# Eight convolution taps of two channel groups as ScalarE products and GpSimd sums

## The chip, the core and the metric

The kernel runs on one core of a Trainium2 chip. Its engines have queues of their own and meet through semaphores: TensorE (PE, with its weight loads PEld), VectorE (DVE), ScalarE (ACT), GpSimd (POOL) and SyncE (SP, which issues the DMAs). The metric is the device time of one launch, in microseconds (us).

## The reference, cut to what matters

Two layers over 256 frames of 1024 channels. In each layer the input projection feeds two things: attention on one half, and on the other half a Conformer convolution module over 512 channels. The part that the change touches is the causal depthwise convolution of width 31:

```
def conformer_conv(u, conv_w, conv_b, ln_g, ln_b):
    a, g = jnp.split(u, 2, axis=-1)
    z = a * jax.nn.sigmoid(g)
    z = lax.conv_general_dilated(
        z, conv_w, window_strides=(1,), padding=[(CONV_WIDTH - 1, 0)],
        dimension_numbers=("NWC", "WIO", "NWC"),
        feature_group_count=D_CONV) + conv_b
    z = layernorm(z, ln_g, ln_b)
    return jax.nn.silu(z)
...
y = jnp.concatenate([y_conv, y_att], axis=-1) @ w_out[l]
x = x + g1[:, None, :] * y
```

Layer 0 then has a dense SwiGLU, layer 1 a top-2-of-8 expert SwiGLU. All data are float32.

## The kernel before

`mix(l, ...)` is the first half of layer `l`: projection, convolution, attention, output projection. Channels lie on the 128 partitions, frames along the free axis. The 512 convolution channels are four groups `a` = 0 to 3 of 128 channels. `glu(a, ps)` takes a projected pair out of PSUM: a sigmoid on ACT (`sg`, line 584) and a product on DVE (line 585) that writes `zp[:, a]`, the padded convolution input. From there each of the 31 taps of a group is one DVE instruction on 128x256: the first a `tensor_scalar` with the bias (line 547), the others `cv = zp shifted * weight + cv` (line 550), with both tensors in SBUF. Of group 3 the last taps (15 in layer 0, 19 in layer 1) are matmuls on PE against diagonal matrices `dgc`, which ACT makes from the identity (line 565); `pe_taps` (line 570) issues them and `pe_done` (line 577) adds their sum.

The whole stretch is under a manual schedule: each engine runs its instructions in the order in which the code is written. The taps are spread by hand. `pump(n)` issues the next `n` taps that are left, taking turns between groups, and `pt(i)` calls it at thirteen marked places with counts from the tables `PUMP0` and `PUMP1`; the `tap` hook puts one tap between the steps of a reciprocal square root in `qk_norm`. What is left is flushed by `pump(4 * CW)` on line 831, ahead of `ln_mean`, where PE averages `cv` over channels (`ps_mu`, line 678).

Between those places stand, in this order: the q and k projections (`ps_q`, `ps_k`) with their norms `qk_norm` (DVE, `qh`), the transposes to `qT` and `kT` (PE `ps_qt`, ACT line 609), the groups 2 and 3 of the convolution input, three blocks of scores (`ps_s`) with their softmax (DVE line 631 gives `s_sb` and the maximum `nm`; ACT line 636 the exponentials), the v projection (`ps_v`), then on ACT the diagonals `dgc`, on PE the transposes `ps_pt`, the taps `ps_cv`, and the weighted sums `ps_o`, which DVE normalises to `o_sb` (line 666). Weights come as 1 MB pieces `raw` by DMA; ACT rounds each to `hi` (line 146) and DVE takes the rest `lo = raw - hi` (line 154, both inputs in SBUF). The four-slot and seven-slot pools `a8` and `a4` hold the larger tiles; `T` is the position bias, loaded by DMA, of which POOL overwrites a corner (line 760).

Of the kernel before, what the change touches and what calls it, by code (L numbers as in the profile page):

```python
# [13 lines left out]
AF = mybir.ActivationFunctionType  # L14
ALU = mybir.AluOpType
AX = mybir.AxisListType

P = 128
D = 1024
S = 256  # L20
# [4 lines left out]
CW = 31  # L25
NE = 8
NPE = (15, 19)
FILL = (1, 1, 1, 0, 1, 10)
NDVE = 9
PT0 = (52, 13, 23, 22)  # L30
PT1 = (29, 49, 15, 36)
RAW = 9
# [21 lines left out]
def kernel(ctx, tc, x, cvec, wada, bada, wga, wqkv, wout, wfgu, wfd, wfd2,  # L54
                      wmgu, wmd, cols, bias, wrt, brt, out):
    nc = tc.nc
# [10 lines left out]
    def bank(name):  # L67
        return pb.tile([P, 512], F32, tag="b", name=name)
# [6 lines left out]
    def sized(tag):  # L75
        def f(name, shape, dt=F32):
            return pools["wk"].tile(shape, dt, tag=tag, name=name, bufs=bufs[tag])
        return f

    a8, a4, a2 = sized("a8"), sized("a4"), sized("a2")  # L80
# [77 lines left out]
    for l in range(2):  # L158
        first = (wqkv[l, 0], wga[l, 0]) if l else (wga[l, 0], wqkv[l, 0])
# [59 lines left out]
    def ahead(nhi, nlo=None, pre=True):  # L219

        for _ in range(nhi):
            if len(his) < limit[0]:
                k, s = halves[len(his)]
                need(k + pre)
                his.append(half_hi(raws[k], s))
            else:
                need(len(raws) + pre)
        for _ in range(nhi if nlo is None else nlo):
            if len(los) < limit[0]:
                k, s = halves[len(los)]  # L230
                los.append(half_lo(raws[k], s, his[len(los)]))
# [50 lines left out]
    ada_raw = []  # L282
    ada_order = [(0, c) for c in (2, 0, 3, 1, 4, 5, 6, 7, 8, 9, 10, 11)] + [(1, c) for c in range(NDVE, 12)]
    ada_done = [0]
# [39 lines left out]
    def ada_through(n):  # L324
        ada_next(n - ada_done[0])
        ada_flush()
# [9 lines left out]
    def ada_steps(l, chs):  # L336

        steps, ws, accs = [], {}, {}

        def fetch(ch):  # L340
            if ch in chs:
                ws[ch] = ada_view(load(wada[l, ch]))

        def part(ch, j):
            if j == 0:
                if ch == chs[0]:
                    fetch(ch)
                accs[ch] = a2("ada_acc", [P, 512])
                nc.vector.tensor_scalar(accs[ch], ws[ch](0), cs[:, 0:1], None, op0=ALU.mult)
            else:  # L350
                if j == 4:
                    fetch(ch + 1)
                nc.vector.scalar_tensor_tensor(accs[ch], ws[ch](j), cs[:, j:j + 1], accs[ch], op0=ALU.mult,  # L353
                                               op1=ALU.add)

        def total(ch):
            ps = bank("ps_adas")
            for g in range(4):
                nc.tensor.matmul(ps[32 * g:32 * g + 32, 0:P], ones_1[:, 0:32], accs[ch][:, g * P:(g + 1) * P],
                                 start=True, stop=True)  # L360
            ada_rows(l, ch, ps)

        for ch in chs:
            for j in range(KT):
                steps.append(lambda ch=ch, j=j: part(ch, j))
                if j == 6 and ch > chs[0]:
                    steps.append(lambda ch=ch: total(ch - 1))
        return steps, lambda: total(chs[-1])
# [14 lines left out]
    def vec(l, v):  # L383
        return vcol[:, l, 2 * v:2 * v + 2, :].rearrange("p a b -> p (a b)")

    def scale_col(l, v, ng, name):
        a = const.tile([P, KT], F32, name=name)
        for q in range(2):
            s = slice(4 * q, 4 * q + 4)
            nc.vector.scalar_tensor_tensor(a[:, s], vec(l, v)[:, s], 1.0, ng[:, s], op0=ALU.add, op1=ALU.mult)  # L390
        return a
# [139 lines left out]
    def mix(l, late, close, hhi, hlo, head=None):  # L531
        zp = a8("zp", [P, 4, S + CW - 1])
        nc.gpsimd.memset(zp[:, :, 0:CW - 1], 0.0)
        cv = a4("cv", [P, 4, S])
        cw = COL["cw", l].rearrange("p (a i) -> p a i", a=4)
        taps, turn = {}, [0]

        def pump(n):

            for _ in range(n):  # L540
                left = [a for a in taps if taps[a]]
                if not left:
                    return
                a = max(left, key=lambda a: (a != turn[0], len(taps[a])))
                turn[0], i = a, taps[a].pop(0)
                if i == 0:
                    nc.vector.tensor_scalar(cv[:, a, :], zp[:, a, 0:S], cw[:, a, 0:1], COL["cb", l][:, a:a + 1],
                                            op0=ALU.mult, op1=ALU.add)
                else:
                    nc.vector.scalar_tensor_tensor(cv[:, a, :], zp[:, a, i:i + S], cw[:, a, i:i + 1], cv[:, a, :],  # L550
                                                   op0=ALU.mult, op1=ALU.add)
# [26 lines left out]

        def pt(i):
            pump((PUMP0, PUMP1)[l][i])  # L580

        def glu(a, ps):
            sg = a2("sg", [P, S])
            nc.scalar.activation(sg, ps[:, 0], AF.Sigmoid)
            nc.vector.tensor_tensor(zp[:, a, CW - 1:], ps[:, 1], sg, op=ALU.mult)
            taps[a] = list(range(CW - NPE[l] if a == 3 else CW))

        def qk_norm(bk):
            ss = sm.tile([P, NT, H], F32, tag="qss", name="qss")
# [50 lines left out]
        def turned(qt, h0, hg, s_sb):  # L640
            nkb = qt + 1
            r = []
            for b0 in range(0, hg * nkb, 4):
                ps = bank("ps_pt").rearrange("p (a s) -> p a s", a=4)
                for a in range(4):
                    h, kb = divmod(b0 + a, nkb)
                    nc.tensor.transpose(ps[:, a, :], s_sb[:, h, kb * P:(kb + 1) * P], ident)
                pT = a2("pT", [P, 4, P])
                nc.scalar.activation(pT, ps, AF.Copy)
                r.append((b0, pT))  # L650
            return r
# [23 lines left out]
        def ln_mean():  # L675
            ps = bank("ps_mu")
            for a in range(4):
                nc.tensor.matmul(ps[:, 0:S], ones_m, cv[:, a, :], start=a == 0, stop=a == 3)
            nc.vector.tensor_tensor(cv, cv, ps[:, None, 0:S].to_broadcast([P, 4, S]), op=ALU.subtract)
            sq = a4("sqc", [P, 4, S])  # L680
            nc.scalar.activation(sq, cv, AF.Square)
            return sq
# [110 lines left out]
        for t in range(NT):  # L793
            nc.scalar.activation(v_sb[:, t, :], bv[t], AF.Copy)
        n0, n1, n2, n3 = (PT0, PT1)[l]
        p0 = turned(*g0, s0)
# [32 lines left out]
        ahead(1, 0)  # L829
        ada_through(6)  # L830
        pump(4 * CW)
        sq = ln_mean()
        ahead(0, 1)
        out_att(wa, (0,))
# [13 lines left out]
    def ffn(hhi, hlo, late):  # L848
# [18 lines left out]

        steps, last = ada_steps(1, range(NDVE))
        total, done = len(steps), [0]
# [511 lines left out]
    def late_mix1():  # L1381
        ada_through(22 - NDVE)
        A, B = scale_col(1, 4, COL["ng2", 1], "A2_1"), vec(1, 3)
        nc.vector.tensor_scalar(A, A, NORM, None, op0=ALU.mult)
        BW = a2("BW", [P, KT, NE])
        for o_, v in ((BW, B), (wrt_sb, A)):
            nc.vector.tensor_tensor(o_, wrt_sb, v[:, :, None].to_broadcast([P, KT, NE]), op=ALU.mult)
        ps = bank("ps_bw")
        nc.tensor.matmul(ps[:, 0:KT * NE], ones_1, BW.rearrange("p j e -> p (j e)"), start=True, stop=True)
        bw = const.tile([P, NE], F32, name="bw")  # L1390
        nc.vector.tensor_reduce(bw, ps[:, 0:KT * NE].rearrange("p (j e) -> p e j", e=NE), axis=AX.X, op=ALU.add)
        nc.vector.tensor_tensor(bw, bw, brt_sb, op=ALU.add)
        return A, B, wrt_sb, bw
# [10 lines left out]
    with tc.manual_schedule():  # L1404
# [45 lines left out]
        ga(w0, *dst, p0, ((0, range(4, 8)), (1, range(8))))  # L1450
        ga(w1, *dst, p1, ((0, range(4, 8)), (1, range(8))))
        mix(0, keep(late_mix0), close_block, *dst, (p0, p1, bq))
        ffn(*dsts[0], keep(late_ffn))
        nc.sync.dma_start(wrt_sb, wrt)
# [3 lines left out]
        def close_mix1(*args):  # L1458
            layer2.append(moe(*args))
            next(layer2[0])  # L1460

        mix(1, late_mix1, close_mix1, *dsts[1])
    next(layer2[0], None)

# [56 lines left out]
```

## Time and profile before

| | us |
|---|---|
| median of 3 runs | 1393.73 (1391.57 to 1395.06) |
| profiled execution | 1396.89 |
| its span, first to last instruction | 1395.2 |
| PE busy | 1322.7 (95%) |
| DVE busy | 772.2 (55%) |
| ACT busy | 371.5 (27%) |
| POOL busy | 3.1 (18 instructions) |

The busy shares are means over the whole span. The two mixes lie at about 47 to 165 us and 387 to 505 us; the rest is the dense SwiGLU between them and the experts behind them. In the rows below a time is counted from the start of the span.

### The profile page before, as it was taken

Reading aid. Unit: us, or ns where it says so; the run is one execution under the profiler, and the core shown is the slowest. Engines: PE = TensorE matmul, PEld = TensorE weight load, DVE = VectorE, ACT = ScalarE, POOL = GpSimd, SP = SyncE. Lnnn points to the kernel's source line nnn. Section 1 sums busy time; section 2 is a strip of 40 time slices with the busy share of each in tenths; the row PEclk is TensorE's granted clock in tenths of the full one; section 3 lists DMA queues with packets and bytes.
Section 4 is the critical chain, followed back from the end, with each engine's and each line's share of the span. In section 5 each row is a group of like instructions: output and inputs, shape, how many; then the busy total and the mean of one; then the engine's idle time right before and its main releaser. Section 6 shows DMA issues by size and latency. Waiting matters only on the chain.

```text
span 1395.2 us, 38875 instructions
## 1 busy us (share of the span) xinstructions
PE 1322.7 (95%) x17220; PEld 974.2 (70%) x17220; DVE 772.2 (55%) x1832; ACT 371.5 (27%) x574; POOL 3.1 (0%) x18
## 2 busy tenths in 40 slices
PE   4998999999899999999899999999999999999996
PEld 4877689999788676666567666766765776666663
DVE  3498677777689855343566565653344343334253
ACT  3336443443455430101234333410000100100000
POOL 0000000000000000000000000000000000000000
PEclk9999999999999999999999999999999999999999
DMA  9962787888461469899879999999999999999995
GB/s 387 399 276 91 262 305 275 307 300 300 161 237 59 151 218 401 353 424 424 344 309 423 387 373 371 367 413 424 424 425 424 424 424 424 396 418 418 423 424 215
DMA packets 66383, 473.64 MB, mean 339 GB/s; under 512 B 7840, under 2 KB 7968, under 8 KB 9248
## 3 DMA queue, kind: packets, MB, share of 16 engines
q1 hardware_dynamic: 66208, 471.09, 83.9%
q8 instruction: 137, 2.24, 0.6%
q14 instruction: 38, 0.31, 0.1%
HBM read 470.01 MB, written 1.05 MB: 338 GB/s over the span
## 4 chain that ended last, share of the span: by engine, by line
PE 81%; DVE 8%; DMA 6%; ACT 4%; issue 1%; SPq 0%; ACTq 0%; DVEq 0%
PE ps_gu L1090 28%; PE ps_d L1090 14%; PE ps_ga L262 4%; PE ps_ga L260 4%; PE ps_ga L261 4%; DMA raw<-in_wmd 3%; DVE lo L154 3%; PE ps_g L1031 2%; PE ps_y L714 2%; PE ps_ada L314 2%; DVE hT L1135 1%; PE ps_f L261 1%; PE ps_f L260 1%; PE ps_f L262 1%; PE ps_gu L262 1%; DMA raw<-in_wmgu 1%
## 5 line engine op out<-in xcount | busy, mean ns | idle before, releaser
L1090 PE MATMUL ps_gu<-raw,xn 128*32 128x256 f32 x8064 | 445.8, 379 | 1.2 <-DVE rt L983 0.6
L1090 PEld LDWEIGHTS ps_gu<-raw,xn 128*32 128x32 f32 x8064 | 279.3, 110 | 156.1 <-issue 2.4
L154 DVE TENSOR_TENSOR lo<-raw,hi 128x2048 fp32r<-128x2048 f32 x99 | 225.4, 2290 | 75.3 <-ACT hi L146 74.3
L1124 DVE TENSOR_TENSOR mh<-ps_gu,sg 128x256 f32<-128x256 f32 (+1 forms) x91 | 32.6, 382 | 368.5 <-ACT sg L1121 368.5
L1090 PE MATMUL ps_d<-raw,hT 128*32 128x256 f32 x4032 | 228.2, 379 | 2.4 <-DMA raw<-in_wmd 2.4
L146 ACT ACTIVATE hi<-raw 128x2048 fp32r<-128x2048 f32 x99 | 188.3, 1913 | 114.4 <-PE ps_ga L262 42.9
L1135 DVE STREAM_TRANSPOSE hT<-mh 32x96 f32<-32x96 f32 (+1 forms) x784 | 200.1, 255 | 13.2 <-PE ps_bc L379 0.2
L1090 PEld LDWEIGHTS ps_d<-raw,hT 128*32 128x32 f32 x4032 | 136.1, 110 | 84.9 <-DMA raw<-in_wmd 3.7
L1121 ACT ACTIVATE sg<-ps_gu 128x256 f32<-128x256 f32 (+1 forms) x91 | 31.9, 351 | 579.7 <-PE ps_gu L1090 511.8
L260 PE MATMUL ps_ga<-hThi,lo 128*128 128x256 f32 x480 | 137.9, 287 | 7.5 <-ACT hThi L452 7.5
L262 PE MATMUL ps_ga<-hTlo,hi 128*128 128x256 f32 x480 | 137.0, 285 | 0.5 <-DVE hTlo L457 0.5
L261 PE MATMUL ps_ga<-hThi,hi 128*128 128x256 f32 x480 | 136.5, 284 | 0.0
L260 PEld LDWEIGHTS ps_ga<-hThi,lo 128*128 128x128 f32 x480 | 93.2, 194 | 8.6 <-ACT hThi L452 8.4
L262 PEld LDWEIGHTS ps_ga<-hTlo,hi 128*128 128x128 f32 x480 | 92.5, 193 | 1.3 <-DVE hTlo L457 1.3
L261 PEld LDWEIGHTS ps_ga<-hThi,hi 128*128 128x128 f32 x480 | 92.8, 193 | 0.2
L550 DVE SCALAR_TENSOR_TENSOR cv<-zp,cols_sb,cv 128x256 f32<-128x256 f32 x206 | 85.6, 482 | 0.0
L262 PE MATMUL ps_gu<-lo,xg 128*128 128x512 f32 x112 | 46.3, 414 | 8.9 <-DVE lo L154 8.9
L260 PE MATMUL ps_gu<-hi,xg 128*128 128x512 f32 x112 | 46.3, 413 | 3.7 <-ACT hi L146 3.7
L353 DVE SCALAR_TENSOR_TENSOR ada_acc<-raw,cs,ada_acc 128x512 f32<-128x512 f32 x63 | 47.3, 750 | 1.2
L261 PE MATMUL ps_gu<-hi,xg 128*128 128x512 f32 x112 | 45.7, 408 | 0.0
L314 PE MATMUL ps_ada<-raw,crep 128*32 128x128 f32 x960 | 34.2, 301 | 7.5 <-DMA raw<-in_wada 7.2
L314 PEld LDWEIGHTS ps_ada<-raw,crep 128*32 128x32 f32 x960 | 28.9, 121 | 11.4 <-issue 8.5
(265 smaller groups left out, 1274.4 us busy)
## 6 DMA issues: line engine op xcount, KB each, us to landing
raw<-in_wmgu SPq DMA_DIRECT2D x222, 1024.0 KB, 13.7
raw<-in_wmd SPq DMA_DIRECT2D x111, 1024.0 KB, 14.3
raw<-in_wada SPq DMA_DIRECT2D x48, 1024.0 KB, 6.6
raw<-in_wfgu SPq DMA_DIRECT2D x22, 1024.0 KB, 5.9
raw<-in_wqkv SPq DMA_DIRECT2D x12, 1024.0 KB, 6.8
raw<-in_wfd SPq DMA_DIRECT2D x11, 1024.0 KB, 6.9
raw<-in_wga SPq DMA_DIRECT2D x8, 1024.0 KB, 11.2
raw<-in_wout SPq DMA_DIRECT2D x8, 1024.0 KB, 7.2
```

Of the source, the lines that this page charges most:

```text
L146: nc.scalar.activation(hi[:, i * w:(i + 1) * w], r, AF.Copy)
L154: nc.vector.tensor_tensor(lo[:, w], r, hi[:, w].bitcast(F32), op=ALU.subtract)
L260: nc.tensor.matmul(o_, a[1], b[0], start=first, stop=False)
L261: nc.tensor.matmul(o_, a[0], b[0], start=False, stop=False)
L262: nc.tensor.matmul(o_, a[0], b[1], start=False, stop=last)
L314: nc.tensor.matmul(ps[32 * g:32 * g + 32, 0:P], crep[:, j, :], w(j)[:, g * P:(g + 1) * P], start=j == 0, stop=j == KT - 1)
L353: nc.vector.scalar_tensor_tensor(accs[ch], ws[ch](j), cs[:, j:j + 1], accs[ch], op0=ALU.mult, op1=ALU.add)
L550: nc.vector.scalar_tensor_tensor(cv[:, a, :], zp[:, a, i:i + S], cw[:, a, i:i + 1], cv[:, a, :], op0=ALU.mult, op1=ALU.add)
L1090: nc.tensor.matmul(ps[t // 2][32 * j:32 * j + 32, t % 2], x(t), w(j), start=first and t % 2 == 0, stop=last, skip_group_check=True)
L1121: nc.scalar.activation(sg[:, 2 * b:2 * b + m, :], v[:, 0:m, 0, :], AF.Silu)
L1124: nc.vector.tensor_tensor(hm[:, 2 * b:2 * b + m, :], v[:, 0:m, 1, :], sg[:, 2 * b:2 * b + m, :], op=ALU.mult)
L1135: nc.vector.transpose(hT[32 * q:32 * q + 32, :, j], v[32 * j:32 * j + 32, :, q])
```

## The change

Of the groups 0 and 1 the last eight taps (`NSIDE`) leave DVE. Each becomes a product on ACT, a copy of shifted `zp` scaled by the tap's weight, into a new tile `side`, which takes one `a4` slot. The first product of a group goes straight to the group's sum `side[:, a]`; the other seven go in turn to two spare quarters, from which POOL adds them to the sum. `pt(i)` now calls `side_taps(2)` behind its `pump`, so that two products (and up to two sums) are issued at each of the first eight places. After the flush DVE adds `side` to `cv` for both groups at once. The counts of `PUMP0` and `PUMP1` stay as they are.

```
+NSIDE = 8
...
+        side, sides = a4("side", [P, 4, S]), []
+
+        def side_taps(n):
+
+            for a, i in sides[:n]:
+                first, q = i == CW - NSIDE, 2 + i % 2
+                nc.scalar.activation(side[:, a if first else q, :], zp[:, a, i:i + S], AF.Copy, scale=cw[:, a, i:i + 1])
+                if not first:
+                    nc.gpsimd.tensor_tensor(side[:, a, :], side[:, a, :], side[:, q, :], op=ALU.add)
+            del sides[:n]
...
         def pt(i):
             pump((PUMP0, PUMP1)[l][i])
+            side_taps(2)
...
-            taps[a] = list(range(CW - NPE[l] if a == 3 else CW))
+            taps[a] = list(range(CW - (NPE[l] if a == 3 else NSIDE if a < 2 else 0)))
+            if a < 2:
+                sides.extend((a, i) for i in range(CW - NSIDE, CW))
...
         pump(4 * CW)
+        side_taps(2 * CW)
+        nc.vector.tensor_tensor(cv[:, 0:2, :], cv[:, 0:2, :], side[:, 0:2, :], op=ALU.add)
         sq = ln_mean()
```

ACT in layer 0, from the sigmoid of group 3 to the diagonals (`warm` reads a tile of ones), before:

```order
L584 ACTIVATE sg<-ps_ga 128x256
L636 ACT_TABLE_LOAD
L636 ACTIVATE s_sb,den<-s_sb,nm 128x128 x8
L636 ACTIVATE s_sb,den<-s_sb,nm 128x256 x8
L790 ACT_TABLE_LOAD
L790 ACTIVATE warm<-ones_90 128x1
L565 ACTIVATE dgc<-ident,cols_sb 128x128 x8
```

and now:

```order
L623 ACTIVATE kT<-ps_qt,cols_sb 128x4x128 x2
L544 ACTIVATE side<-zp,cols_sb 128x256 x2
L596 ACTIVATE sg<-ps_ga 128x256
L650 ACT_TABLE_LOAD
L650 ACTIVATE s_sb,den<-s_sb,nm 128x128 x8
L544 ACTIVATE side<-zp,cols_sb 128x256 x2
L650 ACTIVATE s_sb,den<-s_sb,nm 128x256 x8
L544 ACTIVATE side<-zp,cols_sb 128x256 x2
L804 ACT_TABLE_LOAD
L804 ACTIVATE warm<-ones_90 128x1
L576 ACTIVATE dgc<-ident,cols_sb 128x128 x8
```

Two products stand ahead of the sigmoid, two among the exponentials and two between these and the diagonals. No table load is added.

DVE in layer 0, from the long row of taps to the mean, before:

```order
L550 SCALAR_TENSOR_TENSOR cv<-zp,cols_sb,cv 128x256 x31
L798 RECIPROCAL rden<-den 128x8
L799 RECIPROCAL rden<-den 128x4
L550 SCALAR_TENSOR_TENSOR cv<-zp,cols_sb,cv 128x256 x5
L666 TENSOR_TENSOR o_sb<-ps_o,rden 128x512
L550 SCALAR_TENSOR_TENSOR cv<-zp,cols_sb,cv 128x256 x6
L813 RECIPROCAL rden<-den 128x4
L550 SCALAR_TENSOR_TENSOR cv<-zp,cols_sb,cv 128x256 x9
L334 TENSOR_TENSOR vcol<-ps_adat,bada_sb 128x4
L666 TENSOR_TENSOR o_sb<-ps_o,rden 128x512
L577 TENSOR_TENSOR cv<-cv,ps_cv 128x256
L550 SCALAR_TENSOR_TENSOR cv<-zp,cols_sb,cv 128x256 x3
```

and now:

```order
L561 SCALAR_TENSOR_TENSOR cv<-zp,cols_sb,cv 128x256 x32
L812 RECIPROCAL rden<-den 128x8
L813 RECIPROCAL rden<-den 128x4
L561 SCALAR_TENSOR_TENSOR cv<-zp,cols_sb,cv 128x256 x5
L680 TENSOR_TENSOR o_sb<-ps_o,rden 128x512
L561 SCALAR_TENSOR_TENSOR cv<-zp,cols_sb,cv 128x256 x2
L827 RECIPROCAL rden<-den 128x4
L335 TENSOR_TENSOR vcol<-ps_adat,bada_sb 128x4
L680 TENSOR_TENSOR o_sb<-ps_o,rden 128x512
L588 TENSOR_TENSOR cv<-cv,ps_cv 128x256
L335 TENSOR_TENSOR vcol<-ps_adat,bada_sb 128x4 x2
L847 TENSOR_TENSOR cv<-cv,side 128x512
```

The sixteen taps are gone behind the first `o_sb`; up to there DVE has as many taps as before (the first tap of group 3 has moved to an earlier place). The sum with `side` stands behind the two `vcol`, which before were followed by the subtraction of the mean.

POOL in layer 0 and the start of layer 1, before:

```order
L533 MEMSET zp 128x4x30
L760 MEMSET T 64x8x64
L533 MEMSET zp 128x4x30
L760 MEMSET T 64x8x64
L1293 MEMSET rt 128x3
```

and now:

```order
L534 MEMSET zp 128x4x30
L546 TENSOR_TENSOR side<-side 128x256 x5
L774 MEMSET T 64x8x64
L546 TENSOR_TENSOR side<-side 128x256 x9
L534 MEMSET zp 128x4x30
L546 TENSOR_TENSOR side<-side 128x256 x5
L774 MEMSET T 64x8x64
L546 TENSOR_TENSOR side<-side 128x256 x9
```

Five sums of each layer stand ahead of the write into `T`, nine behind it.

## Rows read from the trace of the kernel before

**Rows 1.** Busy by stage: us, PE, PEld, DVE, ACT, POOL, PEclk, DMA share, GB/s.

```profile
60.40:104.60 44.20, 41.03 (x356) 34.32 (x355) 43.87 (x110) 16.23 (x19) 0.52 (x1) 1.00 0.75 300
104.60:113.80 9.20, 7.77 (x40) 6.04 (x40) 9.13 (x35) 9.01 (x36) 0.00 (x0) 1.00 0.01 3
```

**Rows 2.** Timeline of PE, layer 0: start, us, operation, count [idle before <-releaser].

```profile
78.53 0.66 PE L608 MATMUL ps_qt<-ident,qh 128*128 128x128 f32 x4 [1.10 <-DVE qh L599]
104.36 1.34 PE L622 MATMUL ps_s<-kT,qT 64*128 64x256 f32 x8 [1.60 <-DVE nm L631]
113.80 3.69 PE L570 MATMUL ps_cv<-zp,dgc 128*128 128x256 f32 x16 [1.43 <-issue]
```

**Rows 3.** Timeline of DVE, layer 0: taps, and the reduction in `qk_norm`.

```profile
65.51 4.04 DVE L550 SCALAR_TENSOR_TENSOR cv<-zp,cols_sb,cv 128x256 f32<-128x256 f32 x10
...
86.63 1.28 DVE L593 TENSOR_REDUCE qss<-sq 128x8 f32<-128x512 f32 x2
```

**Rows 4.** Timeline of ACT, layer 0: first and last exponential, then the diagonals.

```profile
104.76 0.40 ACT L636 ACTIVATE s_sb<-s_sb,nm 128x128 f32<-128x128 f32 x1 [7.71 <-DVE nm L633]
...
111.31 0.49 ACT L636 ACTIVATE s_sb<-s_sb,nm 128x256 f32<-128x256 f32 x1
...
113.31 2.44 ACT L565 ACTIVATE dgc<-ident,cols_sb 128x128 f32<-128x128 f32 x8
115.65 1.06 ACT L794 ACTIVATE v_sb<-ps_v 128x512 f32<-128x512 f32 x2
```

**Rows 5.** Timeline of layer 1: group 1's input; remainder ahead of `qk_norm`.

```profile
410.76 0.42 DVE L585 TENSOR_TENSOR zp<-ps_ga,sg 128x256 f32<-128x256 f32 x1 [0.32 <-ACT sg L584]
...
425.07 2.29 DVE L154 TENSOR_TENSOR lo<-raw,hi 128x2048 fp32r<-128x2048 f32 x1 [0.72 <-ACT hi L146]
```

**Rows 6.** Timeline of layer 1: second block's exponentials; the taps on PE.

```profile
446.06 0.51 ACT L636 ACTIVATE s_sb<-s_sb,nm 128x256 f32<-128x256 f32 x1 [2.66 <-DVE nm L633]
...
452.02 2.18 PE L570 MATMUL ps_cv<-zp,dgc 128*128 128x256 f32 x9 [0.89 <-issue]
```

**Rows 7.** Timeline ahead of the mean, layer 0, then layer 1.

```profile
131.78 0.69 DVE L666 TENSOR_TENSOR o_sb<-ps_o,rden 128x512 f32<-128x512 f32 x1 [1.57 <-PE ps_o L661]
...
135.89 0.16 DVE L334 TENSOR_TENSOR vcol<-ps_adat,bada_sb 128x4 f32<-128x4 f32 x1 [0.30 <-PE ps_adat L332]
...
471.13 0.69 DVE L666 TENSOR_TENSOR o_sb<-ps_o,rden 128x512 f32<-128x512 f32 x1 [0.24 <-PE ps_o L661]
472.37 0.27 PE L332 MATMUL ps_adat<-ident,rows 128*128 128x128 f32 x1
472.60 1.59 PEld L678 LDWEIGHTS ps_mu<-cv,ones_m 128*128 128x128 f32 x8 [0.20 <-DVE cv L550]
```

**Rows 8.** DVE's busy time, line 154 alone, then line 550 alone.

```profile
60.40:104.60 44.20, 13.64 (x6) 1.00 0.75 300
...
60.40:104.60 44.20, 21.71 (x50) 1.00 0.75 300
```

**Rows 9.** Timeline of DVE: two SBUF tensors read, then one.

```profile
163.53 0.69 DVE L466 TENSOR_TENSOR x_sb<-x_sb,res 128x512 f32<-128x512 f32 x1
...
168.13 0.75 DVE L425 TENSOR_SCALAR xn<-x_sb,ny 128x1024 f32<-128x1024 f32 x1
```

**Rows 10.** Timeline of POOL: a select, and the write into `T`.

```profile
0.32 0.10 POOL L1511 MEMSET const-float32-0.0<- 128x1 f32 x1 [0.32 <-issue]
...
1.78 0.29 POOL L111 TENSOR_SCALAR_AFFINE_SELECT tri<-ones 128x128 f32<-128x128 f32 x1
...
72.34 0.52 POOL L760 MEMSET T<- 64x512 f32 x1 [70.04 <-DMA T<-in_bias]
```

**Rows 11.** DVE beside that write; PE behind a longer wait; its clock.

```profile
71.73 1.28 DVE L593 TENSOR_REDUCE qss<-sq 128x8 f32<-128x512 f32 x2
...
385.49 1.94 PE L432 MATMUL ps_t<-ident,xn 128*128 128x128 f32 x8 [3.23 <-ACT rows L297]
...
386.00:388.00 2.00, 2.00 (x9) 1.89 (x8) 1.34 (x2) 2.00 (x4) 0.00 (x0) 0.50 0.86 348
```

## The prediction

> **What bounds the kernel now.** The means of the page say little here, so I read the busy time by stage first, then the timeline of each engine at the borders of the stages. In layer 0, from 60.4 to 104.6 us, DVE is busy 43.87 of 44.20 us at a granted clock of 1.00, while PE has gaps [rows 1]; two of PE's waits end with DVE, 1.10 us for `qh` and 1.60 us for the last `nm` [rows 2]. DVE is the bound of that stretch. From 104.6 to 113.8 us ACT is busy 9.01 of 9.20 us [rows 1]: the exponentials start at 104.76 us and the train runs without a gap worth naming to the diagonals at 113.31 us [rows 4]. PE, done with its transposes, waits 1.43 us and starts the taps at 113.80 us [rows 2]. The profile calls that wait "issue", but the first diagonal ends just ahead of it, so I read it as a wait for ACT. From 113.8 us PE leads: DVE waits 1.57 us for `ps_o` before it can make `o_sb` [rows 7]. In layer 1 PE leads through the projections, then a chain over ACT, DVE and PE: DVE waits 0.72 us for `hi` [rows 5] and PE 0.89 us ahead of `ps_cv` [rows 6]. Then PE leads again, with `o_sb` 0.24 us behind `ps_o` [rows 7]. So DVE's time counts in the first part of each mix, ACT's in the middle, and in the last part hardly anything but PE's own.
>
> **What the change takes away.** Sixteen taps leave DVE in each layer, at 4.04 / 10 = 0.40 us each [rows 3]: 6.5 us a layer. But the counts of `pump` are kept, so up to the first `o_sb` DVE does as many taps as before, and all sixteen vanish behind it (the order shows it). There DVE waits for PE anyway [rows 7]. What could be gained is the 0.20 us for which the weight load of `ps_mu` waited for the last taps in layer 1 [rows 7], and it goes with the next item. I count this gain at nothing.
>
> **The sum with `side`.** It is one DVE addition of 128x512 with both inputs in SBUF, 0.69 us by the addition to `x_sb` [rows 9]. In layer 0 it stands behind the `vcol` that starts at 135.89 us, as soon as PE's transpose ahead of `ps_mu` has ended [rows 7], and `ps_mu` now waits for it. Half of the 0.16 us of `vcol` to the next start and 0.69 us: 0.8 us in which PE stands still. In layer 1 it stands behind a `vcol` that needs the transpose of 472.37 to 472.64 us: it ends at about 473.45, where `ps_mu` could start at 472.60. Less the 0.20 us above, 0.7 us.
>
> **The products on ACT.** No row shows one. The diagonals are the same instruction on 128 elements, (115.65 - 113.31) / 8 = 0.29 us each; an exponential goes from 0.40 to 0.49 us from 128 to 256 elements [rows 4]. So 0.29 + 0.1 = 0.4 us, with 0.29 and 0.49 as bounds. Most of the sixteen fall into waits of ACT. Those that don't: in layer 0 four (two among the exponentials, two behind them) stand in the train that ends with the diagonals, 4 x 0.4 = 1.6 us. In layer 1 the two among the exponentials fall into a wait of 2.66 us for `nm` [rows 6], the two behind them do not: 0.8 us. And two stand between `qT` and the `hi` for which DVE waits [rows 5]: 0.8 us, if DVE is there by then.
>
> **The additions on POOL.** Fourteen a layer, and no row shows one of these either. A select of 128x128, which reads one tensor, takes 0.29 us and an empty write 0.10 us, so reading and writing cost (0.29 - 0.10) / 128 = 1.5 ns an element; writing alone, (0.52 - 0.10) / 512 = 0.8 ns by the write into `T` [rows 10]. For 256 elements 0.10 + 256 x 1.5 = 0.48 us with one input, and with a second read at 0.8 ns 0.69 us. I take 0.58 us, the middle. POOL itself has time for fourteen; the write into `T` now stands behind five of them, but these are over well ahead of the softmax that reads `T`, and I cost it at nothing.
>
> The question is what they do to DVE. Of DVE's 44 us in the first stretch of layer 0, 13.64 are remainders and 21.71 taps [rows 8], and both read two SBUF tensors. An operation with two SBUF inputs takes 0.69 us for 512 elements, one with a single input 0.75 us for 1024 [rows 9]: DVE has two streams to read by, and taps use both. If POOL's reads come over one of these, an addition and a tap cannot run at once. The only POOL work beside DVE in the trace is the write into `T` beside a reduction, 1.28 us with it [rows 11] and 1.28 us without [rows 3], but it reads nothing and the reduction has a stream to spare. So the bounds are nothing and the whole addition for each that meets a two-input operation. I take the upper one, since of DVE's rows the taps are nearest to the one that has no stream to spare.
>
> [...]
>
> Place by place in layer 0: the first addition meets the two opening `tensor_scalar` taps (one input) and is free; the second to fifth meet taps, 4 x 0.58; the sixth and seventh meet the taps ahead of `kh`, 2 x 0.58; the next falls on the reduction, free; of the following two one falls on `zp` out of PSUM and one on taps, 0.4. That is 3.9 us, all ahead of the last `nm`, so on the path. In layer 1 the two first products stand ahead of the sigmoid of group 1, whose `zp` DVE already awaits [rows 5]: 0.9 us. The third to seventh additions meet taps, 0.4 + 4 x 0.58 = 2.7 us. Of 3.6 us DVE's wait of 0.72 us takes its share: 2.9 us at the `lo` of 425.07 us, which replaces the 0.8 us by way of `hi`. The rest meet reads from PSUM, or taps behind the last wait.
>
> **Sum.** Layer 0: 3.9 + 1.6 + 0.8 = 6.3 us. Layer 1: 2.9 + 0.8 + 0.7 = 4.4 us. Together 10.7 us. Both mixes run straight into stages that start from their output, so nothing takes this up: the profiled execution, 1396.89 us (span 1395.2, 1.7 us around it), would become 1407.6. That execution was 3.2 us over the median, so I set the sum against the median: 1393.7 + 10.7 = 1404.4 us.
>
> **The rivals.** (1) POOL and DVE do not disturb each other. Then layer 0 costs 1.6 + 0.8 and layer 1 0.8 + 0.8 + 0.7: 4.7 us, 1398.4 us; with products at 0.29 us 3.9 us, 1397.6. For it: no row shows a disturbance. Against it: taps use both streams. (2) The same exclusion, but DVE's unbroken train of taps wins and POOL waits. Then DVE loses little, but a product of ACT waits for the addition that frees its quarter. The place is the last two products of layer 0, ahead of the diagonals: the train of 32 taps behind the softmax lasts 32 x 0.40 = 13 us, to about 121 us, so the diagonals come up to 8 us later still, and some 3 us are lost at the fourth product near 63 us. With the 4.7 us some 15 us: 1409. It decides if POOL does not get in between two taps. (3) On the other side, not slower: PE's 1.43 and 0.89 us are issue time of PE itself, as the profile names them, and not a wait for the diagonals. Then ACT's products hide behind it, 1.43 of 1.6 and all of 0.8 us are saved, and with no disturbance by POOL the sum is 4.7 - 2.2 = 2.5 us; where the sum with `side` meets a late PE it falls to about 1 us: 1395 to 1396 us, no change. It decides if `ps_cv` starts within 0.3 us of where it did. For it speaks the name of the wait, against it the end of the first diagonal. That the taps don't leave DVE is ruled out by the order.
>
> [...]
>
> **How the numbers follow.** Forecast 0.50; rival 1 0.25; rival 2 0.11; rival 3 0.11; a gain, by DVE's freed time in a place that I don't see, 0.03. The range runs from 1396.5 (all but the cheap half of rival 3) to 1411 us (additions at 0.69 us and two falls of the clock, or rival 2). About 0.3%, 4.2 us, is what a measurement of this kernel can tell from no change: above 1397.9 lie the forecast, rival 2 and two thirds of rival 1, 0.77; within it the rest, 0.20; faster 0.03.
>
> **What would show it.** In the changed profile: taps on DVE of over 0.9 us beside POOL's additions (the forecast) or 0.48 us as now (rival 1); additions of several us on POOL and gaps of ACT ahead of `side` (rival 2); `ps_cv` behind a wait of about 3 us in layer 0 (else rival 3); `ps_mu` behind the sum with `side`. I am wrong if the `nm` of layer 0 comes as early as before, or if a later stage takes up the delay.

## The result, and the profile after

The changed kernel takes 1407.55 us (median of 7 executions, 1405.8 to 1411.58); the kernel before, measured beside it, 1393.73 us (7 executions, 1391.57 to 1399.99). The ratio is 1.0092, 95% interval 1.0072 to 1.0112: 13.8 us slower by the medians, 10 to 16 us by the interval. The forecast was 1404.4 us in a range of 1396.5 to 1411.0. The profiled execution took 1408.64 us, 11.75 us more than that of before.

Busy time by stage in the changed kernel, as in [rows 1] (us, PE, PEld, DVE, ACT, POOL, PEclk, DMA share, GB/s; the borders are moved with the work: up to the first exponential's input, then up to `ps_cv`):

```profile
60.90:109.30 48.40, 42.19 (x355) 35.45 (x354) 48.00 (x109) 21.04 (x30) 12.54 (x11) 0.96 0.68 271
109.30:120.20 10.90, 10.85 (x41) 8.33 (x41) 10.82 (x36) 10.66 (x40) 3.73 (x3) 0.70 0.01 2
```

DVE is still busy all the time, but the stretch is 48.40 us long where it was 44.20, with the same amount of work from DVE (109 instructions, before 110); the next is 10.90 where it was 9.20. The timeline of DVE and of POOL, cut to single instructions of layer 0's first row of taps, shows where the 4 us are:

```profile
65.34 0.82 DVE L558 TENSOR_SCALAR cv<-zp,cols_sb 128x256 f32<-128x256 f32 x1
66.08 0.89 DVE L558 TENSOR_SCALAR cv<-zp,cols_sb 128x256 f32<-128x256 f32 x1
66.89 1.03 DVE L561 SCALAR_TENSOR_TENSOR cv<-zp,cols_sb,cv 128x256 f32<-128x256 f32 x1
67.84 0.87 DVE L561 SCALAR_TENSOR_TENSOR cv<-zp,cols_sb,cv 128x256 f32<-128x256 f32 x2
...
66.90 0.74 POOL L546 TENSOR_TENSOR side<-side 128x256 f32<-128x256 f32 x1
70.09 0.82 POOL L546 TENSOR_TENSOR side<-side 128x256 f32<-128x256 f32 x1 [2.45 <-ACT side L544]
```

A tap beside an addition takes 1.03 us, two taps without one 0.87 us together. All taps of the program by operation (count: minimum/median/maximum ns, first and last start):

```profile
L561 DVE SCALAR_TENSOR_TENSOR cv<-zp,cols_sb,cv x174: 468/476/1032, 66.9 to 478.6; 128x256 f32<-128x256 f32 x174
L558 DVE TENSOR_SCALAR cv<-zp,cols_sb x8: 405/616/951, 65.3 to 451.3; 128x256 f32<-128x256 f32 x8
```

Of the 174 taps 17 take 0.78 to 1.03 us, and of the eight opening ones, `tensor_scalar`, four take 0.82 to 0.95 us where 0.41 is usual. So 21 of the 28 additions held DVE, each for 0.3 to 0.56 us, most of them for 0.49. The remainders `lo` read two SBUF tensors as well, but none took over 2.30 us: an addition that came beside one waited for it (last section).

PE in layer 0, answering [rows 2], and PE ahead of `ps_mu` in both layers (timeline):

```profile
81.44 0.33 PE L622 MATMUL ps_qt<-ident,qh 128*128 128x128 f32 x1 [3.55 <-DVE qh L613]
109.12 2.28 PE L636 MATMUL ps_s<-kT,qT 64*128 64x256 f32 x8 [2.48 <-DVE nm L645]
120.16 3.69 PE L581 MATMUL ps_cv<-zp,dgc 128*128 128x256 f32 x16
143.28 1.10 PE L692 MATMUL ps_mu<-cv,ones_m 128*128 128x256 f32 x4 [0.95 <-DVE cv L847]
...
485.87 0.91 PE L692 MATMUL ps_mu<-cv,ones_m 128*128 128x256 f32 x3 [0.85 <-DVE cv L847]
```

PE's waits for `qh` and `nm` have grown by 2.45 and 0.88 us, `ps_cv` starts 6.36 us later and now waits for nothing, and `ps_mu` waits for the sum with `side`. In layer 1 DVE no longer waits for `hi` ahead of the last remainder of [rows 5], but is late itself, and group 1's `zp` waits longer (timeline of DVE, then PE):

```profile
418.85 0.42 DVE L597 TENSOR_TENSOR zp<-ps_ga,sg 128x256 f32<-128x256 f32 x1 [1.60 <-ACT sg L596]
435.89 2.28 DVE L155 TENSOR_TENSOR lo<-raw,hi 128x2048 fp32r<-128x2048 f32 x1
...
444.97 0.88 PE L622 MATMUL ps_qt<-ident,qh 128*128 128x128 f32 x3 [4.40 <-DVE qh L613]
```

The table sets the start times of the same instructions in the traces against those of the kernel before (us later). What a trace was late ahead of anything changed is taken off: in layer 0 the difference that group 1's `zp` already had (0.47 us in the changed kernel), in layer 1 that of group 0's `zp`. `nm` is here that of the third block of scores (108.09 us before). The last two columns belong to two experiments below; rival 1 is the prediction's.

| | forecast | changed | rival 1 | no additions | taps left out |
|---|---|---|---|---|---|
| layer 0: last `nm` | 3.9 | 4.21 | 0 | 0.67 | 0.51 |
| first diagonal | 5.5 | 5.89 | 1.6 | 2.33 | 0.58 |
| second `o_sb` | 5.5 | 6.00 | 1.6 | 2.33 | 0.61 |
| `ps_mu` | 6.3 | 7.11 | 2.4 | 3.44 | 0.61 |
| layer 1: `zp` of group 1 | 0.9 | 1.28 | | 1.28 | -0.28 |
| `ps_qt` of k | 2.9 | 3.98 | 0.8 | 0.80 | -0.28 |
| second `o_sb` | 3.7 | 5.56 | 1.6 | 1.44 | -0.28 |
| `ps_mu` | 4.4 | 6.46 | 2.3 | 2.33 | -0.40 |

The two mixes cost 7.11 + 6.46 = 13.6 us, close to the 13.8 us between the medians. The trace ends only 11.5 us later, mainly since the experts' stage came out 2 us shorter, from 13.43 us late at its first matmul (`ps_gu`) to 11.47 us late at the end. Windows of PE's clock there, before and then after, show a likely reason: a stretch at 0.50 (860 to 862 us) is missing after.

```profile
860.00:880.00 20.00, 20.00 (x273) 15.35 (x275) 7.61 (x12) 7.38 (x12) 0.00 (x0) 0.93 0.80 314
...
873.40:893.40 20.00, 20.00 (x299) 15.03 (x298) 8.46 (x13) 7.92 (x14) 0.00 (x0) 1.00 0.88 347
```

That stage is the same in both kernels, so I don't count this to the change.

### The profile page after: what moved, and what is told of

Its sections match the earlier page's. It is cut to its first block, busy times and chain, and to the rows that moved or that the text cites. A ratio compares the mean times of both kernels' runs of the same rounds, so it can differ in the third digit from the quotient of the medians.

```text
span 1406.7 us, 38933 instructions
## 1 busy us (share of the span) xinstructions
PE 1327.0 (94%) x17220; PEld 987.8 (70%) x17220; DVE 772.1 (55%) x1802; ACT 384.5 (27%) x606; POOL 45.0 (3%) x46
## 4 chain that ended last, share of the span: by engine, by line
PE 77%; DVE 10%; DMA 8%; ACT 3%; issue 1%; SPq 0%; ACTq 0%; DVEq 0%
PE ps_gu L1106 26%; PE ps_d L1106 13%; DMA raw<-in_wmd 5%; PE ps_ga L263 4%; PE ps_ga L261 4%; PE ps_ga L262 4%; DVE lo L155 3%; DVE cv L561 3%; DMA raw<-in_wmgu 2%; PE ps_g L1047 2%; PE ps_y L728 2%; PE ps_ada L315 2%; DVE hT L1151 1%; PE ps_f L261 1%; PE ps_f L262 1%; PE ps_f L263 1%
## 5 line engine op out<-in xcount | busy, mean ns | idle before, releaser
L1106 PEld LDWEIGHTS ps_gu<-raw,xn 128*32 128x32 f32 x8064 | 286.3, 110 | 149.1 <-issue 2.6
L1106 PEld LDWEIGHTS ps_d<-raw,hT 128*32 128x32 f32 x4032 | 139.4, 110 | 82.4 <-DMA raw<-in_wmd 4.3
L561 DVE SCALAR_TENSOR_TENSOR cv<-zp,cols_sb,cv 128x256 f32<-128x256 f32 x174 | 81.6, 522 | 0.5
L546 POOL TENSOR_TENSOR side<-side 128x256 f32<-128x256 f32 x28 | 41.9, 1497 | 186.4 <-ACT side L544 185.3
L315 PE MATMUL ps_ada<-raw,crep 128*32 128x128 f32 x960 | 37.1, 318 | 7.5 <-DMA raw<-in_wada 7.2
## 6 DMA issues: line engine op xcount, KB each, us to landing
raw<-in_wmgu SPq DMA_DIRECT2D x222, 1024.0 KB, 13.8
```

What stands on the lines that cost most here:

```text
L315: nc.tensor.matmul(ps[32 * g:32 * g + 32, 0:P], crep[:, j, :], w(j)[:, g * P:(g + 1) * P], start=j == 0, stop=j == KT - 1)
L546: nc.gpsimd.tensor_tensor(side[:, a, :], side[:, a, :], side[:, q, :], op=ALU.add)
L1106: nc.tensor.matmul(ps[t // 2][32 * j:32 * j + 32, t % 2], x(t), w(j), start=first and t % 2 == 0, stop=last, skip_group_check=True)
```

## The experiments

**Is it POOL's additions, or ACT's reading of `zp` beside the taps?** The additions are left out, the products stay.

```
-                if not first:
-                    nc.gpsimd.tensor_tensor(side[:, a, :], side[:, a, :], side[:, q, :], op=ALU.add)
```

> The changed kernel without the fourteen additions on GpSimd in each layer (of each group only the first product enters the sum); products and the sum at the end stay. My theory, that each addition holds VectorE's operations on SBUF: what the additions cost in the sum, 3.9 us in layer 0 and 2.9 us in layer 1, goes, the 0.8 us by way of `hi` comes back, so 4.7 us over the kernel before: 1398.4 us, and no tap takes over 0.50 us. Rival: the taps are slowed by ScalarE, which reads `zp` beside them: taps of 0.95 us are still there, and the time stays at 1406 to 1408 us.

Measured: 1399.32 us, ratio 1.0032 (1.0019 to 1.0044), that is 4.5 us over the kernel before by the ratio. No tap is held (count: minimum/median/maximum ns):

```profile
L559 DVE SCALAR_TENSOR_TENSOR cv<-zp,cols_sb,cv x174: 453/480/486, 64.7 to 469.1; 128x256 f32<-128x256 f32 x174
```

ACT reads `zp` as before, so it doesn't slow the taps. Against the changed kernel the additions cost 7.11 - 3.44 = 3.7 us in layer 0 and 6.46 - 2.33 = 4.1 us in layer 1, the rest of the table, 5.8 us, is the products, the sum, and, in layer 0, the 0.6 us that its last column has without either (the profiled execution gives some of it back outside the two mixes). PE's wait ahead of `ps_cv` in this run, again named "issue":

```profile
115.32 0.89 PE L579 MATMUL ps_cv<-zp,dgc 128*128 128x256 f32 x3 [3.02 <-issue]
```

It grew from 1.43 to 3.02 us, by the four products' 1.6 us, and PE starts 0.49 us behind the first diagonal (114.83 us), as it did before (113.31 and 113.80 us, [rows 2, 4]): the wait is one for ACT, and rival 3 falls.

**Is it POOL's reading?** Each addition becomes a write.

```
-                    nc.gpsimd.tensor_tensor(side[:, a, :], side[:, a, :], side[:, q, :], op=ALU.add)
+                    nc.gpsimd.memset(side[:, q, :], 0.0)
```

> The changed kernel with each addition on GpSimd replaced by a write of zeros into the product's buffer, so GpSimd is at work at the same moments but reads nothing (the sums are left out of the result). My theory, that it is GpSimd's reading of SBUF that holds VectorE: as without the additions, 1398 to 1399 us, taps at 0.48 us (in the changed kernel the write into `T` from 71.79 us stood beside a tap of 0.48 us). Rival: any work of GpSimd on SBUF holds VectorE for its length: with writes of some 0.3 us for additions that held 0.5 us, some 4 us over that, 1402 to 1403 us, taps of 0.8 us.

Measured: 1399.45 us, ratio 1.0032 (1.0016 to 1.0047), as without additions. POOL's groups, then DVE's taps:

```profile
L546 POOL MEMSET side<- 128x256 f32 x28 | 8.8, 314 | 195.4 <-ACT side L544 194.3
...
L561 DVE SCALAR_TENSOR_TENSOR cv<-zp,cols_sb,cv x174: 454/479/488, 65.2 to 468.6; 128x256 f32<-128x256 f32 x174
L558 DVE TENSOR_SCALAR cv<-zp,cols_sb x8: 405/408/481, 64.6 to 442.8; 128x256 f32<-128x256 f32 x8
```

Twenty-eight writes of 0.31 us, several of them inside rows of taps, hold none of the 174 taps that read two tensors. So it was POOL's reading that held such taps. Of the eight opening taps one, beside a write, took 0.48 us in place of 0.41.

**What does the hold depend on?** One tensor read in place of two, over the same columns; and, in a second kernel, two tensors over half the columns.

```
+                    nc.gpsimd.tensor_scalar(side[:, q, :], side[:, q, :], 1.0, None, op0=ALU.mult)
```
```
+                    nc.gpsimd.tensor_tensor(side[:, a, 0:P], side[:, a, 0:P], side[:, q, 0:P], op=ALU.add)
```

> The changed kernel with each addition on GpSimd replaced by a product with 1.0 of the product's buffer in place, one tensor read in place of two (the sums are left out of the result). My theory, that any reading of SBUF by GpSimd holds VectorE's taps for the whole instruction: taps beside it of 0.8 to 0.95 us, and, as it is a little shorter than the addition, 1404 to 1407 us. Rival: it is the second tensor read that takes VectorE's port, and with one read the taps stay at 0.48 us, 1399 us.

> The changed kernel with each addition on GpSimd over 128 of its 256 columns (the other half of the sums is left out of the result). My theory, that an addition holds VectorE by what it reads: taps beside it some 0.25 us longer than 0.48 us, where the changed kernel has 0.49 us more. Rival: a fixed price of each instruction, 0.49 us as before.

Measured: with one read 1402.05 us (seven executions, 1400.76 to 1406.84), ratio 1.0054 (1.0034 to 1.0074), less than expected; with half the columns, one execution, 1400.33 us beside a median of 1394.72 us. The taps of the first, then of the second:

```profile
L561 DVE SCALAR_TENSOR_TENSOR cv<-zp,cols_sb,cv x174: 451/477/616, 64.3 to 474.0; 128x256 f32<-128x256 f32 x174
...
L546 POOL TENSOR_SCALAR side<-side x28: 845/963/8266, 61.7 to 465.4; 128x256 f32<-128x256 f32 x28
```
```profile
L546 POOL TENSOR_TENSOR side<-side x28: 453/522/8001, 62.4 to 460.8; 128x128 f32<-128x128 f32 x28
...
L561 DVE SCALAR_TENSOR_TENSOR cv<-zp,cols_sb,cv x174: 468/475/729, 65.2 to 469.9; 128x256 f32<-128x256 f32 x174
```

With one read a held tap takes at most 0.62 us, 0.14 more than the median, although the product on POOL itself takes 0.84 us or more, not less than the addition: my expectation of a hold for the whole instruction failed, and so did the rival's 0.48 us. With half the columns the held taps take mostly 0.68 us, 0.20 more. Two reads of 256 columns cost 0.49 us, two of 128 some 0.20, one of 256 0.14. So the hold follows what POOL reads, more than in proportion, and is shorter than POOL's instruction in all three (0.73, 0.45 and 0.84 us at the least). It is neither the fixed price nor the instruction's length. What the two engines share no run shows; the port that the rival names is a guess.

**Do ACT's products lengthen the path to `ps_cv`?** The last four products of each layer move behind the third block of diagonals.

```
-            side_taps(2)
+            side_taps((2, 2, 2, 2, 2, 2, 0, 0, 0, 0, 4, 0, 0)[i])
```

> The changed kernel with its last four products of each layer (two among and two behind the exponentials) moved behind the third block of diagonals; all that is computed stays. My theory, that the products lengthen the train of ScalarE that ends with the diagonals and that PE waits for these: 1.6 us less in layer 0, 0.4 to 0.8 us less in layer 1, and in layer 1 0.5 us less ahead of the first `o_sb`, since no addition meets its taps: 1405 us, `ps_cv` of layer 0 starts 1.6 us earlier against the last `nm`. Rival 3 of the prediction, that PE's wait ahead of `ps_cv` is its own issue time: `ps_cv` stays where it is against the last `nm`, 1407 to 1408 us.

Measured: 1407.66 us (six executions, 1401.67 to 1408.49), ratio 1.0081 (1.0059 to 1.0103). The expected 1405 us did not come; by the time alone this kernel is not to be told from the changed one. The trace, of an execution of 1407.59 us, tells more (timelines of ACT and PE in layer 0, and windows of the clock):

```profile
117.31 0.98 ACT L576 ACTIVATE dgc<-ident,cols_sb 128x128 f32<-128x128 f32 x3
...
111.17 0.63 PE L262 MATMUL ps_v<-hi,hThi 128*128 128x512 f32 x1
118.69 0.49 PE L661 MATMUL ps_pt<-ident,s_sb 128*128 128x128 f32 x3
119.02 0.81 PE L581 MATMUL ps_cv<-zp,dgc 128*128 128x256 f32 x3
...
104.00:108.00 4.00, 1.87 (x9) 1.16 (x7) 3.89 (x18) 0.00 (x0) 0.00 (x0) 0.99 0.35 150
108.00:112.00 4.00, 3.63 (x11) 2.72 (x12) 3.92 (x25) 3.24 (x17) 0.00 (x0) 0.50 0.00 2
```

Against the last `nm` the diagonals come 1.6 us earlier, as expected. But `ps_cv` gains only 0.4 us: behind a wait of 2.50 us for `nm` the granted clock fell to 0.50, a `ps_v` product took 0.63 us for 0.39, and now PE itself comes late. In the changed kernel the same fall follows the wait of 2.48 us (0.50 over 109.2 to 115 us), and PE's transposes end just as the diagonals are ready. Both are late there; with the products moved away, PE's lateness is left. (In layer 1 the third row of `ps_cv` took back 1.7 us: behind a wait of 1.57 us six of its matmuls took 2.81 us, where sixteen of the row before took 3.72.)

**What are the sixteen taps worth?** Left out of the kernel before, with nothing in their place; then left out, with the early counts of `pump` cut.

```
-            taps[a] = list(range(CW - NPE[l] if a == 3 else CW))
+            taps[a] = list(range(CW - (NPE[l] if a == 3 else 8 if a < 2 else 0)))
```
```
-PUMP0 = (4, 8, 2, 6, 5, 10, 1, 32, 5, 6, 9, 60, 23)
-PUMP1 = (0, 10, 5, 7, 2, 0, 11, 24, 13, 7, 13, 30, 34)
+PUMP0 = (0, 6, 0, 4, 3, 6, 1, 32, 5, 6, 9, 60, 23)
+PUMP1 = (0, 8, 3, 5, 0, 0, 4, 24, 13, 7, 13, 30, 34)
```

> The kernel before with the sixteen taps of each layer (eight of group 0, eight of group 1) simply left out, nothing in their place; the counts of `pump` stay. My prediction counts their time at nothing, 0.2 us at most: 1393.5 us. Rival: VectorE's time counts wherever it is saved, 6.5 us a layer: 1381 us.

> The kernel before with the sixteen taps of each layer left out as in the earlier run, and the early counts of `pump` cut by as many (layer 0: 16 fewer ahead of the softmax, layer 1: 15 fewer up to its exponentials), so that VectorE has its free time where it is the bound. Nothing on ScalarE or GpSimd takes their place. My theory, that VectorE's time counts only there and only as far as PE waits for it: in layer 0 the 1.10, 0.26 and 1.60 us of PE's waits go, in layer 1 the 0.89 us ahead of `ps_cv`: 3 to 4 us less than the kernel before, ratio 0.997 to 0.998. This is the most that sixteen taps a layer could bring. Rival: PE is the bound there anyway, and the time is that of the kernel before; or all of the 6.5 us a layer counts, ratio 0.991.

Measured: 1393.92 us, ratio 1.0000 (0.9988 to 1.0011), for the first. With the counts kept, 32 taps fewer are worth nothing. Layer 0 even loses 0.6 us (last column of the table). With the counts cut 1388.01 us, ratio 0.9957 (0.9938 to 0.9976), 6 us; I had expected 3 to 4. The trace has 4.3 us of it in layer 0 and 1.6 us in layer 1. Where most of the 0.6 us go, a timeline of the first of the two shows:

```profile
99.72 0.88 DVE L550 SCALAR_TENSOR_TENSOR cv<-zp,cols_sb,cv 128x256 f32<-128x256 f32 x2
100.12 1.52 DVE L550 SCALAR_TENSOR_TENSOR cv<-zp,cols_sb,cv 128x256 f32<-128x256 f32 x3
```

Two taps take 0.88 us, starting 0.40 us apart; then three take 1.52, 0.52 apart. `pump` alternates between two groups. Groups 0 and 1 are now used up earlier, only group 2 is left, and each tap must wait for the one before it, which writes the same `cv`. This costs 0.3 to 0.4 us, and in the changed kernel the same happens from 105.22 us on. The other 0.2 us come earlier, at `qssv` in `qk_norm`, which took 0.37 us in place of 0.17 while POOL wrote `T` (last section).

**Is the time lost in the kept counts?** The changed kernel with the same cut counts.

> The changed kernel with the early counts of `pump` cut in the same way, all taps still done. My theory, that the kept counts of `pump` leave VectorE's freed time in a place where nobody needs it: PE's waits of 3.55 and 2.48 us in layer 0 and of 4.40 us in layer 1 shrink by what VectorE saves ahead of them (2 to 6 us in layer 0, 2 us in layer 1), while each addition still holds VectorE by 0.5 us: 1399 to 1402 us, still over the kernel before. Rival: the counts don't matter, and the time stays at 1406 to 1408 us.

Measured: 1399.25 us, ratio 1.0030 (1.0015 to 1.0044), 8 us under the changed kernel and still over the one before. In the trace `ps_mu` of layer 0 is 0.5 us earlier than before the change, that of layer 1 2.0 us later. PE's wait for `qh` in layer 0 is gone but for 0.25 us, that in layer 1 shrank from 4.40 to 1.48 us (timeline of PE):

```profile
76.02 1.32 PE L622 MATMUL ps_qt<-ident,qh 128*128 128x128 f32 x8 [0.25 <-DVE qh L613]
...
434.86 1.23 PE L622 MATMUL ps_qt<-ident,qh 128*128 128x128 f32 x8 [1.48 <-DVE qh L613]
```

**The sum with `side` by itself.** It is left out.

```
-        nc.vector.tensor_tensor(cv[:, 0:2, :], cv[:, 0:2, :], side[:, 0:2, :], op=ALU.add)
```

> The changed kernel without the addition of `side` into `cv` ahead of `ps_mu` (the eight taps of groups 0 and 1 are missing from the result; products and additions are done). My theory, that `ps_mu` waits for it, 0.95 us in layer 0 and 0.85 us in layer 1 in the changed kernel: 1.5 to 1.8 us less than the changed kernel, 1405.5 to 1406 us. Rival: the stage behind takes the wait up, no difference.

Measured: 1403.60 us, ratio 1.0064 (1.0042 to 1.0086), under the changed kernel and under what was expected, though the intervals of the two kernels overlap. In the trace `ps_mu` now follows the second `o_sb` by as much as before the change (3.91 us in layer 0, before 3.91; 1.35 in layer 1, before 1.47), where the changed kernel has 5.03 and 2.37. So the sum costs 1.1 and 1.0 us. The rest of the gain is not the sum's: in this trace the second `o_sb` of layer 1 is 0.6 us less late as well, ahead of the place of the sum.

**Does a better placing beat the kernel before?** The change in layer 0 alone, with layer 0's counts cut and its last four products behind the third diagonals, by the edits shown above; and the kernel before with nine taps of layer 0 moved back, nothing else. The second one's edit:

```
-PUMP0 = (4, 8, 2, 6, 5, 10, 1, 32, 5, 6, 9, 60, 23)
+PUMP0 = (2, 7, 0, 5, 4, 8, 1, 32, 5, 6, 13, 60, 23)
```

> The change made in layer 0 alone, with the early counts of `pump` of layer 0 cut by 16 and the last four products behind the third block of diagonals; layer 1 as in the kernel before. My theory: in layer 0 the cut saves some 6 us of VectorE ahead of the last `nm`, the additions take back 3.9 us, the sum with `side` 0.8 us, and the train of ScalarE is as before: 1 to 2 us under the kernel before, ratio 0.9985 to 0.9995. Rival: each addition still costs VectorE more than the tap that it replaces, and the result is at or over the kernel before, ratio 1.000 to 1.003.

> The kernel before with nine taps of layer 0 taken from the early counts of `pump` and done behind the first `o_sb` (four of them ahead of the second `o_sb`); nothing on ScalarE or GpSimd. My theory, that a tap ahead of the last `nm` costs time and one behind the first `o_sb` hardly any: 2 to 3 us less up to `ps_cv`, up to 2 us given back ahead of `ps_mu`, ratio 0.998 to 1.000. Rival: the end of layer 0's mix is as full as its beginning: ratio 1.000 to 1.002.

Measured: the first 1396.34 us, ratio 1.0007 (0.9993 to 1.0022), no difference, so the expected gain of 1 to 2 us did not show; the second 1392.45 us, ratio 0.9979 (0.9966 to 0.9993), 0.2% under the kernel before. In the traces the first gains 1.7 us up to `ps_mu` of layer 0, as expected, and loses 3.1 us between the mixes, where the granted clock was lower than in the kernel before: 0.74 over 170 to 190 us and 0.66 over 382 to 392 us, before 0.83 in both. This trace is of its slowest execution, 1399.67 us, so it stays open how much of the loss the others share. The second gains 2.9 us by `ps_mu` and gives none of it back. Its PE waits (timeline), against [rows 2]:

```profile
101.02 1.34 PE L622 MATMUL ps_s<-kT,qT 64*128 64x256 f32 x8 [0.25 <-DVE nm L631]
110.46 1.75 PE L570 MATMUL ps_cv<-zp,dgc 128*128 128x256 f32 x7 [1.43 <-issue]
```

The wait of 1.60 us for `nm` is down to 0.25, that for `qh` is gone. Nine taps done later, on DVE, bring more in layer 0 (2.9 us by `ps_mu`) than sixteen given to two other engines (1.7 us).

## Why the prediction was right, and where its terms were not

- **The taken taps are worth nothing: right**, and for the reason given, the kept counts (1.0000 with them, 0.9957 without). That the remaining taps of one group would run at 0.52 in place of 0.40 us, 0.3 to 0.4 us ahead of the last `nm`, the step did not see: it counted instructions only.
- **The sum with `side`: right in place, too small.** 1.5 us forecast, 2.1 us measured. The step took the addition's 0.69 us and half a `vcol`; it left out that before, `ps_mu` started without waiting for the second `vcol` at all, and that PE started 0.15 us after the end of the sum.
- **The products on ACT: right.** Two `side` products start 0.40 us apart as forecast. The four in layer 0's train make the diagonals 1.7 us later than `nm` does (forecast 1.6), and without the additions layer 1 has the 0.8 us by way of `hi` (table) and 0.8 us from its last `nm` to the first diagonal. Timeline of ACT in the changed kernel, answering [rows 4]:

```profile
112.61 0.89 ACT L544 ACTIVATE side<-zp,cols_sb 128x256 f32<-128x256 f32 x2
117.34 0.91 ACT L544 ACTIVATE side<-zp,cols_sb 128x256 f32<-128x256 f32 x2
119.67 2.43 ACT L576 ACTIVATE dgc<-ident,cols_sb 128x128 f32<-128x128 f32 x8
```

- **The additions on POOL: the mechanism right, three sizes off.** An addition that waits for nothing takes 0.73 to 0.82 us, not 0.58, but holds a tap for 0.49. Taken as 0.58 for the one and the other, the price was near by luck. The opening `tensor_scalar` taps, counted as free since they read one tensor, are held as well: 0.9 us in layer 0, 1.0 us in layer 1. In layer 0 the two errors cancel, eight holds of 0.49 for the 3.9 us of the forecast; with the 0.3 us of the taps of one group they make the 4.2 us of the table. (The trace without additions differs by 3.5 us only, since there `qssv` was held for 0.37 us by the write into `T`.) In layer 1 they don't: seven holds, 3.5 us, and 1.28 us for the late `zp` (forecast 0.9), less the wait of 0.72 us, give the measured 4.0 us where 2.9 stood. Here, the term of 2.9 us, lies the largest miss.
- **An addition in a long row of taps: left to rival 2, and its price in layer 1 not foreseen.** Two additions waited out a row of taps, as rival 2 had it (timeline of POOL, layer 0 and layer 1):

```profile
117.99 8.81 POOL L546 TENSOR_TENSOR side<-side 128x256 f32<-128x256 f32 x1 [3.14 <-ACT side L544]
...
461.75 7.42 POOL L546 TENSOR_TENSOR side<-side 128x256 f32<-128x256 f32 x1 [5.09 <-ACT side L544]
```

The second got in at the end of the row; it and the one behind it held the taps ahead of the first `o_sb`, which came 0.5 us later still. ACT did wait 2.15 us at the fourth product (the first addition had waited for a remainder), but the `hi` behind it was not late. So in rows of taps rival 2 was true of two additions of 28, and its 8 us at the diagonals did not come, since no product stood behind these additions.
- **The clock: right that it would fall.** The upper end of the range holds two falls; what one costs by itself no run shows, only what ran behind them. The clock fell to 0.50 behind PE's waits for `qh` and `nm` (3.55, 2.48 and 4.40 us); over 109.30 to 120.20 us it was 0.70 in the mean. In layer 0 this was covered by ACT's train, so the forecast's 1.6 us came out although PE by itself would have made 1.3 us of it: with the products moved, `ps_cv` was still 5.5 us late where the last `nm` was 4.2 us late. In layer 1 it was not covered. Behind the wait of 4.40 us, at 0.50 over 445 to 450 us, eight transposes took 1.94 us (1.22 before) and the scores 3.69 us (2.03 before), 2.4 us more together, and DVE had to wait for the third block of scores, which it did not before (timelines of PE and DVE):

```profile
444.97 1.94 PE L622 MATMUL ps_qt<-ident,qh 128*128 128x128 f32 x8 [4.40 <-DVE qh L613]
446.84 3.69 PE L636 MATMUL ps_s<-kT,qT 64*128 64x128 f32 x24
...
457.43 0.42 DVE L645 CUSTOM_DVE_ANT_0 s_sb<-ps_s,T 128x256 f32<-128x256 f32 x1 [0.59 <-PE ps_s L636]
```

So layer 1's last `nm` is 4.69 us late where `ps_qt` of k was 3.98. The first diagonal is 5.08 us late: the products behind the exponentials add only 0.4 us there, not 0.8. With 0.5 us for the additions behind the row of taps and 0.9 us for the sum this gives the 6.5 us of the table, where 4.4 stood.
- **The signs named ahead:** taps of over 0.9 us beside additions, `ps_mu` behind the sum: seen. `ps_cv` behind 3 us: seen only without the additions (3.02). Rival 1 is what remains when POOL doesn't read: 1398.4 us forecast, ratio 1.0032, or 1398.2 us on the same median.
- **Three figures do not come out of the prediction's own rows.** Two products at 0.4 us make 0.8, not 0.9 us, for the late `zp`. All of rival 3, 1395 to 1396 us, lies under the lower end of the range, 1396.5, not its cheap half. Additions at 0.69 us come to about 1405.7, so the two falls of the clock would have to bring 5.3 us to reach the upper end, 1411; rival 2 comes to 1409. The measured 1407.55 us lies under that as well.

What was held and what was not, by the traces: taps with two inputs (up to 1.03 us, median 0.48) and opening `tensor_scalar` taps (up to 0.95 us for 0.41) were held, a reduction took 0.67 us with the addition of 90.03 us beside it and 0.67 us without, `zp` out of PSUM took 0.42 us beside the addition of 99.88 us and 0.42 us without, and writes held no tap of two inputs (at most 0.49 us). The prediction's two streams are my reading of rows: 512 elements of one tensor are reduced in 0.64 us [rows 3], of two added in 0.69 [rows 9]. By it an operation with one input had a stream to spare, but the opening taps were held all the same. The holds of 0.49 and 0.14 us belong to instructions of 0.73 and 0.84 us. Two additions waited out 21 and 18 taps that started after them.

## What to carry to other kernels

An addition that POOL makes in place of a DVE tap cost DVE 0.49 us here where the tap cost 0.40, so in a kernel like this work given to POOL frees DVE only if it meets operations that it does not hold (here reductions, 0.67 us with an addition beside them or not, and `zp` out of PSUM, 0.42 us), or falls into DVE's own waits. Before moving work off a busy engine, look where the saved time comes free: with the order's counts kept, it came free behind the last wait, and 32 taps fewer changed nothing. Moving nine taps past the place where PE waits for DVE brought 0.2% with no new work at all.

## What the runs showed of the hardware

- POOL's hold on DVE was shorter than its instruction and grew with what it read: 0.49 us of at least 0.73 (two tensors, 256 columns), 0.20 of 0.45 (two, 128 columns), 0.14 of 0.84 (one, 256 columns), none for a write of 0.31 us beside taps of two inputs. Why the first is more than twice the second stays open. (The one with one tensor is also another operation, a `tensor_scalar`; the two were not told apart.)
- In the other direction POOL waited: six additions that came while a remainder `lo` ran ended 0.59 to 0.60 us behind its end and took 0.82 to 2.74 us in all, and these remainders took their usual 2.28 us. Where POOL had come first, a remainder was held too: one took 2.41 us beside an operation with one tensor, one 2.48 us beside additions of half the columns. Timeline of two additions, the first of them waiting, and of the remainder:

```profile
99.88 3.56 POOL L546 TENSOR_TENSOR side<-side 128x256 f32<-128x256 f32 x2 [8.70 <-ACT side L544]
...
99.74 2.28 DVE L155 TENSOR_TENSOR lo<-raw,hi 128x2048 fp32r<-128x2048 f32 x1
```

- A write by POOL still held DVE in places: without the additions, `qssv`, a `tensor_scalar` of 128x16, took 0.54 us in place of 0.17 while POOL wrote `T`; with the taps left out it took 0.37 us in layer 0 and 0.58 in layer 1, beside the same write (timeline of the former kernel):

```profile
72.22 0.52 POOL L772 MEMSET T<- 64x512 f32 x1 [69.92 <-DMA T<-in_bias]
72.24 0.54 DVE L607 TENSOR_SCALAR qssv<-qss 128x16 f32<-128x16 f32 x1
```

- Most additions got in ahead of the next tap or the one after; two waited out some 20 taps that started after them, until taps of one group alone came 0.51 us apart (layer 0, from 125.75 us) or the reciprocals came (layer 1, 468.51 us). Of the additions that met a row with more taps to come, these two arrived behind seven or more taps that had run without a hold, the others behind at most six. Kernels with one read or half the columns show the same two places (7.2 and 8.3 us; 6.8 and 8.0 us). What decides it was not tried and stays open.
- Taps on one `cv` group followed each other at 0.52 us, taps on two groups in turn at 0.40 us.
